# The last output product of the last token block: its K tiles in another order

## The chip, the cores and the metric

The kernel runs on one NeuronCore of one Trainium2 chip. The metric is the device time of one execution in microseconds (us), lower is better. TensorE (PE in the profile) does the matrix products into PSUM, which has eight banks of 128 x 512 float32; VectorE (DVE) and ScalarE (ACT) work on the results; GpSimd (POOL) and SyncE (SP) mostly issue transfers (DMAs) here.

## The reference

A decoder trunk of two layers on 2048 tokens of 1024 channels: an mLSTM layer, then an RG-LRU layer, each added to its input, and a last RMSNorm. The change lies in the end of the second layer. Cut to that:

```python
def rglru_mixer(u, w_in, conv_w, conv_b, w_a, b_a, w_x, b_x, lam, w_out):
    ...
    r = sigmoid(xb @ w_a + b_a)            # gates: blocks of 192 channels
    ig = sigmoid(xb @ w_x + b_x)
    log_a = -LRU_C * r * softplus(-lam)
    a = exp(log_a)
    bt = sqrt(-expm1(2.0 * log_a)) * (ig * xc)
    hs = linear_scan(a, bt)                # along the tokens
    y = hs * silu(g)                       # 1536 channels
    return y @ w_out                       # the output product: 1536 -> 1024
...
x = x + y                                  # residual
return rmsnorm(x, final_g)                 # over the 1024 channels of a token
```

## The kernel before

Phases `phase_a1`, `phase_a2` and `phase_b1` compute the mLSTM layer and the input product of the RG-LRU layer, and leave in HBM: the convolved input `xr`, the gate `g`, the residual `x1`, and the weights, already split in two. The change lies in `phase_b2`, which does the rest.

**Data.** Channels lie on the 128 partitions and tokens along the free dimension. A block is 512 tokens (`TB`), there are four (`NTB`). A float32 product is made of three matmuls in a faster format: `mm3` (L357) multiplies the high part of the weights by the high part of the data (L359), by the low part (L360), and the low part of the weights by the high part of the data (L361). High and low parts come from `split_into` (L756): a cast on ACT (L759) and a subtraction on DVE (L762).

**The two jobs.** For each block, `gates` works on four groups of 384 channels, `p` = 0 to 3. A group has six gate sums on PE (tile `gate`), tanh, exp and square root on ACT, the scan and some products on DVE, and ends with three K tiles of the data `y`, as a pair of tiles `yh` and `yl` (L1480 to L1483). So group 3 gives K tiles 9 to 11 of the output product. `x2_out` is the output product of a block, 12 K tiles (`NT`) to 1024 channels, in two halves of 512 channels. A half has four accumulators `acc` of one PSUM bank each (`m` = 0 to 3). One K tile of one half takes 12 matmuls (four `m` by the three of `mm3`) and one weight tile `wr` of 512 KB, fetched from HBM (`d_ow`). After the twelfth K tile of a half, for each `m`: the residual is loaded into `x2` on the SP queue (L1520) and the sum is added to it (L1521, DVE), it is squared (L1525 or L1528, ACT), and the squares are added up in `sacc` (L1532, DVE). After both halves, `stats_sum` (L1096) sums the squares over the channels (L1101, PE; L1104, DVE; L355, POOL), `stats_rows` (L1106) spreads the result (L1111, PE), eight products (L1547, DVE) scale the block, and it is written out (L1548).

**In the last half of the last block** K tiles 9 to 11 are held until all three are there, and are then done accumulator by accumulator, nine matmuls each, so that the accumulators end one after the other. Its last square isn't added to `sacc` but goes to `stats_sum` by itself.

**The order.** The list `steps` is written out by code: per time step one half of a group's gates, then three K tiles of the output product, five time steps (`lag`) behind. Each job is a generator, and the loop at the end of `phase_b2` resumes them in this order. In the last block's product, call the K tile steps by their place in this row, 0 to 23: places 0 to 2 stand behind the second half of the gates of group 2, places 3 to 5 and 6 to 8 behind the two halves of those of group 3, and from place 9 on there are no gates left. Before the change places 0 to 11 are K tiles 0 to 11 of half 0, and places 12 to 23 those of half 1. `weights` (L1387) hands out the weight tiles in the order of the same list, copied as `order`, and fetches up to three ahead; `wr` has four buffers, so the tile of place j goes where that of place j - 4 was. The SP queue issues in order: a transfer that has to wait holds up all behind it. `x2` has eight buffers, so a block's residual can be loaded only when the outputs of the block before it have left them.

This is the order that the code asks for. The framework's scheduler lists each engine's instructions from it, by priorities and its own idea of when things are ready, and can move an instruction ahead of its neighbours. What it made of it stands in the section on the change.

Of the kernel before, what the change touches and what calls it, by code (L numbers as in the profile page):

```python
# [14 lines left out]
P = 128  # L15
# [4 lines left out]
NTB = T // TB  # L20
# [286 lines left out]
class Trunk:  # L307
# [1052 lines left out]
    def phase_b2(self, D, outT):  # L1360
# [3 lines left out]
        NT = 12  # L1364
        with ExitStack() as ctx:
# [3 lines left out]
            pm = ctx.enter_context(tc.tile_pool(name="psB", bufs=8, space=PSUM, reuse_waits="tile"))  # L1369
            steps = []  # L1370
            lag = 5
            for t in range(8 * NTB + lag):
                if t < 8 * NTB:
                    steps.append(("g", t // 8, t % 8))
                if t >= lag:
                    steps += [("r", (t - lag) // 8, (t - lag) % 8 * 3 + i) for i in range(3)]
            order = list(steps)
            ready = []

            def fetch(kind, b, i):  # L1380

                m = 768 if kind == "g" else 512
                both = (gp if kind == "g" else wp).tile([P, 2 * m], F32R, tag="w" + kind, name="w" + kind)
                nc.sync.dma_start(both.bitcast(F32), D["gw" if kind == "g" else "ow"][i])
                return both[:, 0:m], both[:, m:2 * m]

            def weights():  # L1387

                while order and len(ready) < 3:
                    if order[0][0:2] == ("g", 0) and len(ready) == 2:  # L1390
                        break
                    with tc.high_priority(offset=80 if order[0][0:2] == ("r", 0) else None):
                        ready.append(fetch(*order.pop(0)))
                return ready.pop(0)

            def psum(name):
                return pm.tile([P, TB], F32, tag="mm", name=name)
# [101 lines left out]
            def x2_out(b):  # L1499

                bs = slice(b * TB, (b + 1) * TB)
                ys = blocks[b]
                x2, sacc = [], None
                for half in range(2):
                    acc = [psum("acc") for _ in range(4)]
                    last = b == NTB - 1 and half == 1
                    held = []
                    for k in range(NT):
                        held.append((k, weights()))
                        if not last or k < NT - 3 or k == NT - 1:  # L1510
                            for m in range(4):
                                ms = slice(m * P, (m + 1) * P)
                                for i, (wh, wl) in held:
                                    self.mm3(acc[m], wh[:, ms], wl[:, ms], ys[i][0], ys[i][1], i == 0, i == NT - 1)
                            held = []
                        if k < NT - 1:
                            yield
                    for m in range(4):
                        x = tp.tile([P, TB], F32, tag="x2", name="x2", bufs=8)
                        nc.sync.dma_start(x, D["x1"][half * 4 + m, :, bs])  # L1520
                        nc.vector.tensor_tensor(x, x, acc[m], op=ALU.add)  # L1521
                        x2.append(x)
                        if sacc is None:
                            sacc = tp.tile([P, TB], F32, tag="sacc", name="sacc", bufs=1)
                            nc.scalar.activation(sacc, x, AF.Square)  # L1525
                        else:
                            sq = tp.tile([P, TB], F32, tag="sq", name="sq")
                            nc.scalar.activation(sq, x, AF.Square)  # L1528
                            if last and m == 3:
                                sums = [sacc, sq]  # L1530
                            else:
                                nc.vector.tensor_tensor(sacc, sacc, sq, op=ALU.add)  # L1532
                                sums = [sacc]
                    yield
                rc = tp.tile([P, 4], F32, tag="rc", name="rc")
                yield
                yield
                self.stats_sum(tp, pm, sums, rc, "mm")
                yield
                yield  # L1540
                yield
                rb = self.stats_rows(pm, rc, "mm")
                if not last:
                    pb, rb = rb, tp.tile([P, TB], F32, tag="rb", name="rb", bufs=1)
                    nc.scalar.copy(rb, pb)
                for m in range(KD):
                    nc.vector.scalar_tensor_tensor(x2[m], x2[m], self.v("gf", m), rb, op0=ALU.mult, op1=ALU.mult)  # L1547
                    (nc.gpsimd if not last else nc.scalar if m % 2 else nc.sync).dma_start(outT[m, :, bs], x2[m])  # L1548
                    if m % 2:
                        yield  # L1550

            run = {}
            for kind, b, i in steps:
                if kind == "g":
                    if i == 0:
                        run["g", b] = block(b)
                    next(run["g", b])
                else:
                    if i == 0:
                        run["r", b] = x2_out(b)  # L1560
                    next(run["r", b])
                    if b > 0:
                        next(run["r", b - 1], None)
# [99 lines left out]
```

## Time and profile before

| | |
|---|---|
| time, median of 3 runs | 2966.92 us (2966.56 to 2970.99) |
| the profiled execution's own time | 2962.73 us |
| its span in the trace | 2960.7 us |
| mean granted TensorE clock in it | 0.987 of full speed |
| PE busy | 2850.7 us, 96% |
| DVE busy | 2124.2 us, 72% |
| ACT busy | 1516.8 us, 51% |

The profile is one execution, so a sum made from it is a sum against 2962.73 us, of which the trace's span covers all but 2.03 us. Times in its rows are us from the span's start, and buffer numbers are left out of names. A row of the timeline reads: start, duration, engine, line, operation, output<-inputs, count, and in brackets the engine's idle time ahead of it and what ended it. Matmuls overlap: each is shown with some 0.39 us, while the next starts 0.23 us after it. A row of the waits reads: engine, tile and line, what released it, us in total, times, the longest. In a row of the windows stand the stretch, its length, each engine's busy time with the count of its instructions, the granted clock of PE (PEclk, 1.00 is full speed), the busy share of the DMA engines and GB/s. SPq rows are transfers at the moment when SP issues them; the listing of transfers gives for each kind the count, the size and the median us from issue to landing.

### The profile page before, as it was taken

Reading aid. Unit: us, or ns where it says so; the run is one execution under the profiler, and the core shown is the slowest. Engines: PE = TensorE matmul, PEld = TensorE weight load, DVE = VectorE, ACT = ScalarE, POOL = GpSimd, SP = SyncE. Lnnn points to the kernel's source line nnn. Section 1 sums busy time; section 2 is a strip of 40 time slices with the busy share of each in tenths; the row PEclk is TensorE's granted clock in tenths of the full one; section 3 lists DMA queues with packets and bytes.
Section 4 is the critical chain, followed back from the end, with each engine's and each line's share of the span. In section 5 each row is a group of like instructions: output and inputs, shape, how many; then the busy total and the mean of one; then the engine's idle time right before and its main releaser. Section 6 shows DMA issues by size and latency. Waiting matters only on the chain.

```text
span 2960.7 us, 43267 instructions
## 1 busy us (share of the span) xinstructions
PE 2850.7 (96%) x15442; PEld 2440.3 (82%) x15442; DVE 2124.2 (72%) x3584; ACT 1516.8 (51%) x2545; POOL 445.8 (15%) x846
## 2 busy tenths in 40 slices
PE   7999999999999899999999799999999999999997
PEld 5799987889987798999999777887788887777885
DVE  7766789535668588888888755778889466766763
ACT  6354556324445466666666533435345233967761
POOL 1211122101123111111111201101221111000000
PEclk9999999999999999999999899999999999999998
DMA  6766677668889656465656568685776666878855
GB/s 228 262 227 231 239 255 269 193 200 305 267 315 314 220 166 211 142 205 171 205 185 215 213 234 285 219 264 186 257 254 210 218 199 202 293 248 306 300 193 171
DMA packets 294839, 686.58 MB, mean 232 GB/s; under 512 B 29024, under 2 KB 107616, under 8 KB 294624
## 3 DMA queue, kind: packets, MB, share of 16 engines
q1 hardware_dynamic: 227440, 450.34, 47.5%
q0 software_dynamic: 66608, 232.43, 20.9%
q8 instruction: 121, 1.98, 0.3%
q10 hardware_dynamic: 576, 1.05, 0.1%
q14 instruction: 94, 0.77, 0.1%
HBM read 446.53 MB, written 237.17 MB: 231 GB/s over the span
## 4 chain that ended last, share of the span: by engine, by line
PE 35%; DVE 12%; issue 6%; ACT 4%; DMA 1%; POOL 1%; SPq 0%; DVEq 0%; POOLq 0%; ACTq 0%
PE pa L361 2%; PE pa L359 2%; PE pa L360 2%; PE pd L360 2%; PE pd L359 2%; PE pd L361 2%; PE pc L359 2%; PE pc L360 2%; PE pc L361 2%; PE acc L360 2%; PE acc L361 2%; PE acc L359 2%; DVE Cl L762 2%; PE pb L360 1%; PE pb L361 1%
## 5 line engine op out<-in xcount | busy, mean ns | idle before, releaser
L759 ACT CAST s<-raw 128x512 fp32r<-128x512 f32 (+1 forms) x280 | 172.5, 620 | 260.6 <-PE pd L361 70.6
L762 DVE TENSOR_TENSOR s<-raw,s 128x512 fp32r<-128x512 f32 (+1 forms) x280 | 191.4, 688 | 63.9 <-ACT s L759 62.8
L359 PE MATMUL acc<-yh,wr 128*128 128x512 f32 x384 | 151.2, 402 | 15.6 <-DMA wr<-d_ow 8.3
L360 PE MATMUL acc<-yl,wr 128*128 128x512 f32 x384 | 152.8, 398 | 0.6 <-DVE yl L762 0.6
L361 PE MATMUL acc<-yh,wr 128*128 128x512 f32 x384 | 152.1, 396 | 0.0
L759 ACT CAST u<-t 128x512 fp32r<-128x512 f32 x112 | 68.8, 619 | 159.1 <-PE pc L361 49.8
L686 DVE SCALAR_TENSOR_TENSOR xc<-xm,vec,xc 128x512 f32<-128x512 f32 x192 | 139.1, 746 | 6.9 <-ACT xc L684 6.1
L762 DVE TENSOR_TENSOR u<-t,u 128x512 fp32r<-128x512 f32 x112 | 76.7, 689 | 88.4 <-ACT u L759 87.9
L759 ACT CAST s<-sum 128x512 fp32r<-128x512 f32 (+1 forms) x120 | 74.0, 618 | 117.5 <-PE pc L361 46.4
L359 PE MATMUL pa<-u,s 128*128 128x512 f32 x304 | 122.7, 403 | 4.6 <-ACT p L258 3.1
L361 PE MATMUL pa<-u,s 128*128 128x512 f32 x304 | 121.8, 401 | 0.5 <-DVE s L762 0.5
L360 PE MATMUL pa<-u,s 128*128 128x512 f32 x304 | 122.0, 401 | 0.0
L759 ACT CAST Ch<-C 128x516 fp32r<-128x516 f32 x120 | 74.8, 623 | 86.7 <-DVE da L1010 59.6
L992 DVE SCALAR_TENSOR_TENSOR C<-C,dl,kv 128x516 f32<-128x516 f32 x112 | 83.3, 744 | 47.6 <-PE kv L361 47.6
L686 DVE SCALAR_TENSOR_TENSOR xc<-xr,vec,xc 128x512 f32<-128x512 f32 x144 | 105.8, 747 | 9.2 <-ACT xc L684 8.1
L359 PE MATMUL pj<-vwh,xmh 128*128 128x512 f32 x256 | 102.6, 401 | 1.9 <-ACT vwh L759 1.8
L359 PEld LDWEIGHTS acc<-yh,wr 128*128 128x128 f32 x384 | 72.6, 190 | 36.5 <-issue 8.7
L360 PE MATMUL pj<-vwl,xmh 128*128 128x512 f32 x256 | 99.9, 390 | 1.3 <-DVE vwl L762 1.3
L762 DVE TENSOR_TENSOR s<-sum,s 128x512 fp32r<-128x512 f32 (+1 forms) x120 | 82.5, 688 | 25.6 <-ACT s L759 24.8
L361 PE MATMUL pj<-vwh,xml 128*128 128x512 f32 x256 | 100.1, 391 | 0.0
L360 PE MATMUL pd<-u,s 128*128 128x512 f32 x224 | 88.6, 395 | 1.3 <-DVE u L762 1.3
L359 PE MATMUL pd<-u,s 128*128 128x512 f32 x224 | 88.3, 394 | 0.0
(479 smaller groups left out, 10012.5 us busy)
## 6 DMA issues: line engine op xcount, KB each, us to landing
wr<-d_ow SPq DMA_DIRECT2D x96, 512.0 KB, 4.4
d_wx<-s POOLq DMA_DIRECT2D x64, 512.0 KB, 4.4
s<-d_wx SPq DMA_DIRECT2D x64, 512.0 KB, 4.4
s<-d_ws SPq DMA_DIRECT2D x64, 512.0 KB, 6.3
raw<-in_wxz_dram SPq DMA_DIRECT2D x124, 256.0 KB, 5.0
d_wr<-s POOLq DMA_DIRECT2D x48, 512.0 KB, 3.7
s<-d_wr SPq DMA_DIRECT2D x48, 512.0 KB, 4.3
wg<-d_gw SPq DMA_DIRECT2D x32, 768.0 KB, 4.9
```

Of the source, the lines that this page charges most:

```text
L359: mm(out, sh, mh, start=first, stop=False, skip_group_check=resumed)
L360: mm(out, sh, ml, start=False, stop=False, skip_group_check=resumed)
L361: mm(out, sl, mh, start=False, stop=last, skip_group_check=resumed)
L686: nc.vector.scalar_tensor_tensor(out, x[:, j:j + TB], self.v(wn, m * 4 + j), out, op0=ALU.mult, op1=ALU.add)
L759: a = nc.scalar.copy(hi, src)
L762: b = (nc.gpsimd if lo_eng == "p" else nc.vector).tensor_tensor(lo, src, hi.bitcast(F32), op=ALU.subtract)
L992: nc.vector.scalar_tensor_tensor(C2, C2, self.dl[:, r:r + 1], p2, op0=ALU.mult, op1=ALU.add)
```

## The change

In the last block the output product takes its K tiles in the order: tiles 0 to 8 of half 0 (places 0 to 8, as before), tiles 0 to 8 of half 1 (places 9 to 17), tiles 9 to 11 of half 0 (18 to 20), tiles 9 to 11 of half 1 (21 to 23, held as before). `turn` maps the place to half and K tile. Both halves' accumulators are then open at once, eight banks, and the end of half 0 (residual, squares, sums) comes right ahead of half 1's held tiles. The other blocks keep their order. No instruction is added or left out.

```diff
+            def turn(b, i):
+
+                if b < NTB - 1 or i < NT - 3:
+                    return i
+                return i + 3 if i < 2 * NT - 6 else i - (NT - 3) if i < 2 * NT - 3 else i
...
-                    steps += [("r", (t - lag) // 8, (t - lag) % 8 * 3 + i) for i in range(3)]
+                    steps += [("r", (t - lag) // 8, turn((t - lag) // 8, (t - lag) % 8 * 3 + i)) for i in range(3)]
...
-                for half in range(2):
-                    acc = [psum("acc") for _ in range(4)]
-                    last = b == NTB - 1 and half == 1
-                    held = []
-                    for k in range(NT):
-                        held.append((k, weights()))
-                        if not last or k < NT - 3 or k == NT - 1:
-                            for m in range(4):
-                                ms = slice(m * P, (m + 1) * P)
-                                for i, (wh, wl) in held:
-                                    self.mm3(acc[m], wh[:, ms], wl[:, ms], ys[i][0], ys[i][1], i == 0, i == NT - 1)
-                            held = []
-                        if k < NT - 1:
-                            yield
+                last = b == NTB - 1
+                accs = {}
+                held = []
+                for j in range(2 * NT):
+                    half, k = divmod(turn(b, j), NT)
+                    if k == 0:
+                        accs[half] = [psum("acc") for _ in range(4)]
+                    acc = accs[half]
+                    held.append((k, weights()))
+                    if not last or half == 0 or k < NT - 3 or k == NT - 1:
+                        for m in range(4):
+                            ms = slice(m * P, (m + 1) * P)
+                            for i, (wh, wl) in held:
+                                self.mm3(acc[m], wh[:, ms], wl[:, ms], ys[i][0], ys[i][1], i == 0, i == NT - 1)
+                        held = []
+                    if k < NT - 1:
+                        yield
+                        continue
...
-                            if last and m == 3:
+                            if last and half == 1 and m == 3:
```

What the scheduler made of it, first on PE at place 9 (the numbers tell buffers apart: `wr_28106` is the weight tile of place 9 in both kernels, `wr_28156` before that of place 12; `acc_27902` to `acc_27905` are half 0, `acc_28207` to `acc_28210` half 1 before, `acc_28142` to `acc_28145` half 1 after; `yh_28084` and `yl_28085` are the data of group 3, `yh_27534` and `yl_27535` of group 0). Before:

```order
L361 MATMUL acc_27905<-yh_27898,wr_28088 128x512
L359 MATMUL acc_28207<-yh_27534,wr_28156 128x512
L359 MATMUL acc_27902<-yh_28084,wr_28106 128x512
L359 MATMUL acc_27903<-yh_28084,wr_28106 128x512
L359 MATMUL acc_27904<-yh_28084,wr_28106 128x512
L360 MATMUL acc_27902<-yl_28085,wr_28106 128x512
L361 MATMUL acc_27902<-yh_28084,wr_28106 128x512
```

After:

```order
L361 MATMUL acc_27905<-yh_27898,wr_28088 128x512
L359 MATMUL acc_28142<-yh_27534,wr_28106 128x512
L360 MATMUL acc_28142<-yl_27535,wr_28106 128x512
L361 MATMUL acc_28142<-yh_27534,wr_28106 128x512
L359 MATMUL acc_28143<-yh_27534,wr_28106 128x512
L360 MATMUL acc_28143<-yl_27535,wr_28106 128x512
```

Before, one matmul of place 12 stood ahead of place 9, and behind it place 9, which reads group 3. Now place 9 is the first K tile of half 1, which reads group 0, and the places follow each other in their own order up to the last.

On SP the places of the transfers stay the same, and only what is fetched changes. From the weight tile of place 9 to that of place 13, before (`x2` is the residual, half 0's from `x2_28184`, half 1's from `x2_28375`):

```order
L1384 DMA wr_28106<-d_ow_95 128x1024
L1520 DMA x2_28184<-d_x1_85 128x512
L1520 DMA x2_28189<-d_x1_85 128x512
L1520 DMA x2_28195<-d_x1_85 128x512
L1520 DMA x2_28201<-d_x1_85 128x512
L1384 DMA wr_28124<-d_ow_95 128x1024
L1520 DMA x2_28375<-d_x1_85 128x512
L1384 DMA wr_28142<-d_ow_95 128x1024
L1520 DMA x2_28381<-d_x1_85 128x512
L1520 DMA x2_28387<-d_x1_85 128x512
L1384 DMA wr_28156<-d_ow_95 128x1024
L1520 DMA x2_28393<-d_x1_85 128x512
```

After:

```order
L1390 DMA wr_28106<-d_ow_95 128x1024
L1530 DMA x2_28314<-d_x1_85 128x512
L1530 DMA x2_28319<-d_x1_85 128x512
L1530 DMA x2_28325<-d_x1_85 128x512
L1530 DMA x2_28331<-d_x1_85 128x512
L1390 DMA wr_28124<-d_ow_95 128x1024
L1530 DMA x2_28375<-d_x1_85 128x512
L1390 DMA wr_28146<-d_ow_95 128x1024
L1530 DMA x2_28381<-d_x1_85 128x512
L1530 DMA x2_28387<-d_x1_85 128x512
L1390 DMA wr_28160<-d_ow_95 128x1024
L1530 DMA x2_28393<-d_x1_85 128x512
```

The tiles of places 9 to 12 are `wr_28106`, `wr_28124`, `wr_28142` (after: `wr_28146`) and `wr_28156` (after: `wr_28160`), in this order in both. The residual loads stand between them as before.

On DVE, the end of half 0 and the first accumulator of half 1 (`x2_28375`). Before:

```order
L1521 TENSOR_TENSOR x2_28201<-x2_28201,acc_27905 128x512
L1532 TENSOR_TENSOR sacc_28187<-sacc_28187,sq_28192 128x512
L1532 TENSOR_TENSOR sacc_28187<-sacc_28187,sq_28198 128x512
L1532 TENSOR_TENSOR sacc_28187<-sacc_28187,sq_28204 128x512
L1521 TENSOR_TENSOR x2_28375<-x2_28375,acc_28207 128x512
L1532 TENSOR_TENSOR sacc_28187<-sacc_28187,sq_28378 128x512
```

After:

```order
L1531 TENSOR_TENSOR x2_28331<-x2_28331,acc_27905 128x512
L1542 TENSOR_TENSOR sacc_28317<-sacc_28317,sq_28322 128x512
L1542 TENSOR_TENSOR sacc_28317<-sacc_28317,sq_28328 128x512
L1531 TENSOR_TENSOR x2_28375<-x2_28375,acc_28142 128x512
L1542 TENSOR_TENSOR sacc_28317<-sacc_28317,sq_28334 128x512
L1542 TENSOR_TENSOR sacc_28317<-sacc_28317,sq_28378 128x512
```

One addition to `sacc` has gone behind the first addition of half 1; the rest stands as before. ACT and POOL keep their order.

## The prediction

> **What bounds the kernel now.** I read the page first, then PE's waits over the whole span, then the timeline and the windows around the one wait that lies in the changed product.
>
> ```profile
> span 2960.7 us, 43267 instructions
> PE 2850.7 (96%) x15442; PEld 2440.3 (82%) x15442; DVE 2124.2 (72%) x3584; ACT 1516.8 (51%) x2545; POOL 445.8 (15%) x846
> ...
> PE pt L1045 <- ACT hh L1035: 13.9, 3, 11.7
> PE ssum L1101 <- DVE acc L498: 13.6, 1, 13.6
> PE acc L359 <- DMA wr<-d_ow: 8.3, 1, 8.3
> ```
>
> PE is busy for 96% of the span, so time comes from what PE waits for and from nothing else, unless the end is touched. The third wait is the output product's, and it happened once. The two above it lie in other phases. In PE's timeline the wait is this:
>
> ```profile
> 2892.72 0.40 PE L361 MATMUL acc<-yh,wr 128*128 128x512 f32 x1
> 2901.41 2.04 PE L359 MATMUL acc<-yh,wr 128*128 128x512 f32 x4 [8.29 <-DMA wr<-d_ow]
> ...
> 2904.41 0.39 PE L361 MATMUL acc<-yh,wr 128*128 128x512 f32 x1
> ...
> 2944.38 0.40 PE L361 MATMUL acc<-yh,wr 128*128 128x512 f32 x1
> ```
>
> The row at 2892.72 is the last matmul of place 8. The order of before has behind it one matmul of place 12 and then place 9, so PE stood for two things at once: the weights of place 12 and the data of group 3. The two engines that make that data, and the SP queue with the weights:
>
> ```profile
> 2897.36 1.47 ACT L759 CAST yh<-g 128x1536 fp32r<-128x1536 f32 x1 [1.60 <-DVE g L1479]
> ...
> 2898.87 1.76 DVE L762 TENSOR_TENSOR yl<-g,yh 128x1536 fp32r<-128x1536 f32 x1 [1.54 <-ACT yh L759]
> ...
> 2860.76 19.31 SPq L1384 DMA_DIRECT2D wr<-d_ow  x6
> 2885.18 3.79 SPq L1520 DMA_DIRECT2D x<-d_x  x4
> 2889.07 0.40 SPq L1384 DMA_DIRECT2D wr<-d_ow  x1
> 2890.36 0.32 SPq L1520 DMA_DIRECT2D x<-d_x  x1
> 2890.78 0.45 SPq L1384 DMA_DIRECT2D wr<-d_ow  x1
> 2891.57 2.55 SPq L1520 DMA_DIRECT2D x<-d_x  x2
> 2894.21 0.38 SPq L1384 DMA_DIRECT2D wr<-d_ow  x1
> 2895.66 0.32 SPq L1520 DMA_DIRECT2D x<-d_x  x1
> 2906.00 27.97 SPq L1384 DMA_DIRECT2D wr<-d_ow  x11
> ```
>
> The group of six ends with the tile of place 9, issued at about 2879.7; the three single ones are places 10, 11 and 12; the eleven are places 13 to 23. The listing of transfers gives their times to landing, for places 9, 10, 11 and 12 in this order, and the last row is that of all issued from 2895 on:
>
> ```profile
> wr<-d_ow SPq DMA_DIRECT2D x1, 512.0 KB, 3.4
> ...
> wr<-d_ow SPq DMA_DIRECT2D x1, 512.0 KB, 7.7
> ...
> wr<-d_ow SPq DMA_DIRECT2D x1, 512.0 KB, 7.9
> ...
> wr<-d_ow SPq DMA_DIRECT2D x1, 512.0 KB, 7.1
> ...
> DMA to landing us min/median/max: 3.4/3.6/5.1
> ```
>
> So place 9 landed at 2883.1, place 10 at 2896.8, place 11 at 2898.7 and place 12 at 2894.21 + 7.1 = 2901.3. PE went on at 2901.41, 0.1 us behind that last one: the weights of place 12 ended the wait. But the data was hardly earlier: `yh` was there at 2898.83, `yl` at 2900.63.
>
> **What goes.** The stretches of that product by windows, of the instructions on `acc` alone:
>
> ```profile
> 2884.60:2893.00 8.40, 8.40 (x36) 6.59 (x35) 0.00 (x0) 0.00 (x0) 1.00 0.91 288
> 2893.00:2901.40 8.40, 0.12 (x1) 0.02 (x1) 0.00 (x0) 0.00 (x0) 0.76 0.93 354
> 2901.40:2904.40 3.00, 2.99 (x7) 2.40 (x8) 0.00 (x0) 0.00 (x0) 0.52 0.00 0
> 2904.40:2944.80 40.40, 40.38 (x174) 32.40 (x172) 4.81 (x7) 0.00 (x0) 1.00 0.46 143
> ```
>
> First the pause. In the first window 36 matmuls take 8.40 us, 0.233 each, so place 9 could have begun at 2892.72 + 0.23 = 2892.95. It began at 2901.41: 8.46 us. Second, the clock behind the pause: for 3.00 us PE was granted 0.52 of full speed, which costs 3.00 x 0.48 = 1.44 us. A second way to the same number: places 9 to 23 are 180 matmuls, 41.9 us at 0.233 each, and took from 2901.41 to 2944.61, 43.2 us. Together 9.9 us hang on this wait.
>
> **What comes.** After the change place 9 needs only the weights that landed at 2883.1 and data of group 0, which is long there; its four banks were last read by the gates on ACT, the last of them here:
>
> ```profile
> 2884.79 0.69 ACT L1441 ACTIVATE ig<-gate,lc 128x512 f32<-128x512 f32 x1
> ```
>
> That ends at 2885.5, 7 us before. So place 9 runs from 2892.95 to 2895.74 (12 x 0.233). Place 10 needs weights that were issued behind four residual loads and landed at 2896.8; PE went on 0.1 us behind a landing above, so it starts at 2896.87: a new wait of 1.13 us. Nothing about that transfer changes, since SP's places are the same and up to 2892.95 all engines do what they did. I take 1.13 us. Behind it on PE stand only the places that follow, and DVE and ACT have nothing of this product to do until half 0 ends, so the wait moves the end by its own length. Its bounds: nothing, if the load takes the 3.4 us of place 9's (landing at 2892.5), and 1.3 us if it takes place 11's 7.9.
>
> [...]
>
> Places 11 and 12 come at 2896.87 + 2.79 = 2899.66 and 2902.45, and their weights are there at 2898.7 and 2901.3. The loads of places 13 and 14 move forward: SP waited with them for a free buffer, and places 9 and 10 now free theirs at some 2896 and 2899.8. Landing after 3.6 to 7.9 us, they are there from 2899.6 to 2903.9 and from 2903.4 to 2907.7; PE wants them at 2905.24 and 2908.03. That holds, but at the long end by 1.3 and 0.3 us only, which is where I look for trouble. From place 15 on the stretch is quiet again (median 3.6) and a tile has three K tiles of time, 8.4 us. The last tile is issued at 2906.00 + 27.97 - 0.32 = 2933.65 before and lands at 2937.25, and the held matmuls want it at 2944.61 - 30 x 0.233 = 2937.6; its distance to the tiles ahead of it doesn't change, so neither does that. Half 0's residuals are loaded as early as before and only wait longer in their buffers, which nobody wants any more.
>
> What a short wait does to the clock shows in an earlier place, where the data of the group before came late:
>
> ```profile
> 2797.37 1.20 PE L359 MATMUL acc<-yh,wr 128*128 128x512 f32 x4 [0.90 <-ACT yh L759]
> 2798.41 0.39 PE L360 MATMUL gate<-xcl,wg 128*128 128x512 f32 x1
> ```
>
> Four matmuls take 1.04 us instead of 0.93: 0.1 us behind a pause of 0.90. I take 0.1 here too.
>
> Group 3's data is wanted at place 18, at 2892.95 + 1.13 + 0.1 + 9 x 2.79 = 2919.3, 18.7 us behind `yl`. Even if the gates' chain got slower by that much, it would cost nothing.
>
> **The end.** Half 0's end now lies right ahead of half 1's. What DVE does in both, before:
>
> ```profile
> 2909.49 2.77 DVE L1521 TENSOR_TENSOR x<-x,acc 128x512 f32<-128x512 f32 x4 [8.87 <-PE acc L361]
> 2912.19 2.28 DVE L1532 TENSOR_TENSOR sacc<-sacc,sq 128x512 f32<-128x512 f32 x3
> 2938.55 0.69 DVE L1521 TENSOR_TENSOR x<-x,acc 128x512 f32<-128x512 f32 x1 [24.08 <-PE acc L361]
> 2939.99 0.69 DVE L1532 TENSOR_TENSOR sacc<-sacc,sq 128x512 f32<-128x512 f32 x1 [0.76 <-ACT sq L1528]
> 2940.63 0.69 DVE L1521 TENSOR_TENSOR x<-x,acc 128x512 f32<-128x512 f32 x1
> ...
> 2944.82 0.69 DVE L1521 TENSOR_TENSOR x<-x,acc 128x512 f32<-128x512 f32 x1
> ```
>
> Half 0's last accumulator was done at about 2911.5; DVE had its four additions behind it 0.7 us later and the first two of `sacc` 2.0 us later. Half 1's first accumulator is done 9 x 0.233 = 2.1 us later, when DVE is just free for it. From there on a round of DVE is 2940.63 - 2938.55 = 2.08 us, and PE's nine matmuls are 2.1 us, so the two keep step as before; the addition to `sacc` that was put behind the first addition of half 1 fills the 0.76 us in which DVE waited for ACT. So the end costs 0 to 0.1 us. Its other bound is a slip by one addition and its wait, 0.69 + 0.76 = 1.45 us, since a chain without slack never makes good a delay. Everything behind 2944.82 is as before.
>
> **Sum.** -8.46 - 1.44 + 1.13 + 0.1 + 0.1 = -8.6 us. Against the profiled execution's own 2962.73 us (span 2960.7) that is 2954.1. The median of the three runs is 4.2 us above the profiled one, by something that the profile doesn't show; applied to the median the forecast is 2966.92 - 8.6 = 2958.3 us, -0.29%. About 0.2%, 5.9 us, is what a measurement of this kernel can tell from no change.
>
> **Rivals.**
>
> A second wait behind the first. If the forward moved loads of places 13 and 14 land later than any seen here, because they join the crowded stretch earlier, PE waits again. With 7.9 + 3.6 = 11.5 us for place 13, issued at 2896, it lands at 2907.5 and costs 2.3 us: -6.3 us. If that pause also brings the slow clock, 1.44 us more: -4.9 us, 2962.0, no difference that can be told. For it speaks the margin of 0.3 us; against it that the traffic that made 7.9 us ends by itself (the window from 2901.40 on has no transfer at all). Chance 0.14.
>
> A shorter pause in ordinary runs. The profiled execution may have had place 12's weights late. But without that, place 9 of before still had to wait for `yh` at 2898.83: a pause of 5.9 us at least. Then -5.9 - 1.44 + 1.13 = -6.2 us or a little more, 2960.7. It also covers that the wait was put down to the wrong thing: whichever of weights or data it was, it goes. Chance 0.12.
>
> The end slips by one step: -8.6 + 1.4 = -7.2 us, 2959.7. Chance 0.06.
>
> Slower: the clock. If several short waits in a row (places 10, 13, 14) brought PE to the 0.52 seen behind the long pause, again and again, half of the 168 matmuls from place 10 on would take 1.92 times as long: 84 x 0.233 x 0.92 = 18 us more, and -8.6 becomes +9.4, 2976.3. All of them would be 36 us; slower by over 0.2% begins at 8.6 + 5.9 = 14.5 us of loss, with 40% of them slow. Against it: behind the 0.90 us pause the rows show 0.1 us of loss, and the windows 1.00 with PE busy throughout. [...] Chance 0.03.
>
> **How the numbers follow.** The forecast as worked out has what is left, 0.65. Faster by over 0.2%: nearly all of that (0.62), most of the slipping end (0.05), and about half of the shorter pause and a third of the second wait (0.11): 0.78. Slower by over 0.2%: the clock and a little that I don't see, 0.04. The rest, 0.18, is no difference. The range: at the low end 9.8 us, all that goes and no new wait, against the profiled execution's own time, 2952.9; at the high end the second wait with the slow clock, 2962.0, and 1 us of the runs' scatter: 2953 to 2963.
>
> **What would show it.** Right: in PE's waits the 8.3 us for `wr` is gone, and one of some 1.1 us stands near 2895.8; PEclk is 1.00 from 2893 on; PE's last matmul on `acc` starts near 2935.8 instead of 2944.38; DVE's last addition follows it within 0.1 us. Wrong: a wait of over 2 us on `wr` at places 13 or 14, a clock below 0.9 between 2893 and 2935, a gap between PE's last matmul and DVE's last addition, or a span that shrinks by less than 6 us.

## The result, and the profile after

Over five runs each, the changed kernel took 2956.82 us in the median (2954.88 to 2958.55) against 2966.92 us (2965.79 to 2972.34) for the one before: a ratio of 0.9965, with an interval of 0.9954 to 0.9975. It is faster by 0.35%. Run again later beside other kernels, it came to 2954.07 us and a ratio of 0.9961 (0.9949 to 0.9974). The forecast was 2958.3 us, faster.

The page of the kernel after: span, engines and the clock granted to TensorE.

```profile
span 2955.1 us, 43268 instructions
...
PE 2851.6 (96%) x15442; PEld 2440.9 (83%) x15442; DVE 2124.6 (72%) x3584; ACT 1517.0 (51%) x2545; POOL 445.5 (15%) x846
...
PEclk9999999999999999999999999999999999999999
```

PE's busy time is what it was (2850.7 before). The span is 5.6 us shorter, so waiting went away and not work. PE's waits in the last 255 us (columns: who waited for what, sum, times, longest):

```profile
PE acc L359 <- ACT yh L759: 0.9, 1, 0.9
PE acc L359 <- DMA wr<-d_ow: 0.9, 2, 0.6
```

The one wait of 8.3 us for weights has become two that make 0.9 us together; the wait for `yh` lies in an earlier block and stands in both kernels. PE's timeline has the two new ones, and the first and last row of the stretch that the change reaches:

```profile
2895.40 0.39 PE L361 MATMUL acc<-yh,wr 128*128 128x512 f32 x1
...
2898.19 0.39 PE L361 MATMUL acc<-yh,wr 128*128 128x512 f32 x1
...
2899.19 0.50 PE L359 MATMUL acc<-yh,wr 128*128 128x512 f32 x1 [0.61 <-DMA wr<-d_ow]
2899.53 0.39 PE L360 MATMUL acc<-yl,wr 128*128 128x512 f32 x1
...
2931.94 0.50 PE L359 MATMUL acc<-yh,wr 128*128 128x512 f32 x1 [0.29 <-DMA wr<-d_ow]
...
2938.78 0.40 PE L361 MATMUL acc<-yh,wr 128*128 128x512 f32 x1
```

2895.40 is the last matmul of place 8. Place 9 follows it without a gap and ends with the matmul at 2898.19; place 10 begins at 2899.19, behind its weights. The row at 2931.94 is where the held tiles begin (places 21 to 23). From here on I measure the changed product by one number, **the stretch**: from the start of place 8's last matmul to the start of the last matmul on the accumulators. 180 matmuls lie in it, 41.8 us at their usual distance of 0.232. Before, it was 2944.38 - 2892.72 = 51.66 us; after, 2938.78 - 2895.40 = 43.38 us. That is 8.28 us gained.

The window over the stretch (us, then busy time of PE, PEld, DVE and ACT, the clock, the DMA engines' share, GB/s) shows what became of the stage at 0.52:

```profile
2895.60:2939.10 43.50, 42.60 (x181) 33.47 (x179) 4.82 (x7) 0.00 (x0) 1.00 0.59 201
```

Full clock throughout. The tile of place 10 in SP's queue, its landing, and the transfers issued from 2898 on (min, median, max):

```profile
2887.86 4.04 SPq L1530 DMA_DIRECT2D x<-d_x  x4
2892.00 0.60 SPq L1390 DMA_DIRECT2D wr<-d_ow  x1
...
2898.61 29.18 SPq L1390 DMA_DIRECT2D wr<-d_ow  x11
```

```profile
wr<-d_ow SPq DMA_DIRECT2D x1, 512.0 KB, 7.1
...
DMA to landing us min/median/max: 4.1/4.3/7.2
```

2892.00 + 7.1 = 2899.1, and PE went on at 2899.19. The tile of place 23 is the last of the eleven: issued at 2898.61 + 29.18 - 0.32 = 2927.47 (its issue took 0.32), wanted by the held tiles, which went on at 2931.94, 4.5 us behind the issue. The end, on DVE:

```profile
2934.39 0.69 DVE L1542 TENSOR_TENSOR sacc<-sacc,sq 128x512 f32<-128x512 f32 x1 [0.16 <-ACT sq L1538]
2935.04 0.69 DVE L1531 TENSOR_TENSOR x<-x,acc 128x512 f32<-128x512 f32 x1
2936.49 0.69 DVE L1542 TENSOR_TENSOR sacc<-sacc,sq 128x512 f32<-128x512 f32 x1 [0.76 <-ACT sq L1538]
...
2939.22 0.69 DVE L1531 TENSOR_TENSOR x<-x,acc 128x512 f32<-128x512 f32 x1
```

DVE's last addition starts 0.04 us behind PE's last matmul (2938.78 + 0.40). From PE's last matmul on `acc` to the end of the span there are 16.3 us before and after (16.6 when the changed kernel was run again).

One thing doesn't fit at first sight: the stretch lost 8.28 us, the span 5.6. The rest lies ahead of the stretch, in instructions that the change leaves in place: place 8 ended 2.68 us later than in the execution before. One of the waits that differ there, in the time up to 2885 us, of before and of after:

```profile
PE acc L359 <- ACT ig L1441: 0.7, 2, 0.4
```

```profile
PE acc L359 <- ACT ig L1447: 2.3, 2, 1.9
```

In all eleven experiments, some built from the kernel before and some from the one after, this wait is 2.1 to 2.3 us. So the 0.7 of before was luck in the one execution that was profiled. Over the thirteen profiles place 8's last matmul starts anywhere from 2891.1 to 2896.9 us. That scatter of 5.8 us, not the change, makes spans of single executions differ, and it is why the experiments are read by the stretch first.

### The profile page after: what moved, and what is told of

Its sections match the earlier page's. It is cut to its first block, busy times and chain, and to the rows that moved or that the text cites. A ratio compares the mean times of both kernels' runs of the same rounds, so it can differ in the third digit from the quotient of the medians.

```text
span 2955.1 us, 43268 instructions
## 1 busy us (share of the span) xinstructions
PE 2851.6 (96%) x15442; PEld 2440.9 (83%) x15442; DVE 2124.6 (72%) x3584; ACT 1517.0 (51%) x2545; POOL 445.5 (15%) x846
## 4 chain that ended last, share of the span: by engine, by line
PE 35%; DVE 12%; issue 6%; ACT 4%; DMA 1%; POOL 1%; DVEq 0%; POOLq 0%; SPq 0%; ACTq 0%
PE pa L361 2%; PE pa L359 2%; PE pa L360 2%; PE pd L360 2%; PE pd L359 2%; PE pd L361 2%; PE pc L359 2%; PE pc L360 2%; PE pc L361 2%; PE acc L360 2%; PE acc L361 2%; PE acc L359 2%; DVE Cl L762 2%; PE pb L360 1%; PE pb L361 1%
```

## The experiments

**The theory.** In the kernel before, PE stood behind place 8 for two things on top of each other: the data of group 3, and, through one matmul of place 12 that the scheduler had put ahead of place 9, the weights of place 12. The data is the cause, and the change works because nine tiles lie between. The first rival is that the weights are the cause, late because SP put residual loads ahead of them. The second is that the slow clock behind the pause comes from something other than the idle time, so that it would be there without it. All ratios are to runs of the kernel before on the same chip.

| kernel | stretch, us | ratio (interval) |
|---|---|---|
| before (its profile) | 51.66 | 1 |
| before, place 12's matmul in its place | 50.87 | 0.9997 (0.9988 to 1.0007) |
| before, 36 more matmuls in the pause | 50.25 | 0.9997 (0.9987 to 1.0006) |
| before, residual loads late | 48.13 | 0.9990 (0.9981 to 1.0000) |
| before, data of group 3 not needed | 42.98 | 0.9971 (0.9961 to 0.9980) |
| after, one tile of half 1 first | 46.76 | 0.9987 (0.9978 to 0.9996) |
| after, three tiles of half 1 first | 42.62 | 0.9968 (0.9956 to 0.9980) |
| after | 43.38 | 0.9965 (0.9954 to 0.9975) |
| after, run again | 43.14 | 0.9961 (0.9949 to 0.9974) |
| after, residual loads late | 41.83 | 0.9968 (0.9957 to 0.9979) |
| the same, run again | 41.83 | 0.9971 (0.9960 to 0.9981) |
| after, five weight buffers | 41.83 | 0.9954 (0.9940 to 0.9968) |
| after, residual loads late, five buffers | 41.83 | 0.9959 (0.9946 to 0.9971) |

**1. Before, without the early matmul of place 12.** It is tied behind the last matmul of place 11 (`mm3` here returns its first and its last matmul, and `order` puts the second argument behind the first).

```diff
+ a = self.mm3(acc[m], wh[:, ms], wl[:, ms], ys[i][0], ys[i][1], i == 0, i == NT - 1)
+ if b == NTB - 1 and (half, i) == (1, 0):
+     self.order((ended,), a[0:1])
+ if half == 0:
+     ended = a[1]
```

> The kernel before, with an order set between two matmuls: the first of place 12 may not stand ahead of place 11's last. Nothing else moves. I read the stretch S from the start of place 8's last matmul to the start of the product's last one: 51.66 us before, 43.38 after the change, 41.8 (180 x 0.232) without any wait. My theory is that place 9 stood for two things at nearly the same time, the weights of place 12 (8.7 us behind place 8) and the data of group 3 (6.2 us behind it). Then taking the early matmul away wins the difference only: a pause of some 6.0 us for the ACT cast and the slow clock behind it, S = 41.8 + 6.0 + 1.4 = 49.2, 2.5 us less than before. Rival, the weights alone: places 9 to 11 have theirs in time but for some 1 us, S = 42 to 44. Rival, the data alone: no change, 51.7.

PE's timeline where the pause ends, and the windows behind it:

```profile
2902.46 2.07 PE L359 MATMUL acc<-yh,wr 128*128 128x512 f32 x4 [5.77 <-ACT yh L760]
```

```profile
2902.40:2904.50 2.10, 2.04 (x5) 1.41 (x6) 0.00 (x0) 0.00 (x0) 0.50 0.81 322
2904.50:2906.00 1.50, 1.50 (x5) 1.21 (x5) 0.00 (x0) 0.00 (x0) 0.50 0.05 18
2906.00:2910.00 4.00, 4.00 (x13) 3.11 (x13) 0.00 (x0) 0.00 (x0) 0.67 0.19 47
2910.00:2947.50 37.50, 37.50 (x162) 29.88 (x160) 4.81 (x7) 0.00 (x0) 1.00 0.48 149
```

Without the weights the wait stays, now for `yh`, and is 2.5 us shorter, as expected. But the stretch gained only 0.8 us, since the slow clock lasted until some point between 2906 and 2910, where it had lasted 3.0 us. From 2902.46 on the 179 distances took 44.71 us instead of 41.56: 3.15 us lost to the clock, against 1.41 before by the same working. The rival by which the weights alone hold PE is out.

**2. Before, with data that is there.** In half 0 of the last block, K tiles 9 to 11 read the data of K tiles 0 to 2. Thus 512 channels of 512 tokens aren't the reference's.

```diff
- self.mm3(acc[m], wh[:, ms], wl[:, ms], ys[i][0], ys[i][1], i == 0, i == NT - 1)
+ y = ys[i - 9 if b == NTB - 1 and half == 0 and i > 8 else i]
+ self.mm3(acc[m], wh[:, ms], wl[:, ms], y[0], y[1], i == 0, i == NT - 1)
```

> The kernel before, in the old order, but in the last block K tiles 9 to 11 of half 0 multiply the data of K tiles 0 to 2 in place of their own, so 512 output channels of 512 tokens aren't the reference's; the work and the transfers are the same. PE then never has to wait for group 3 at place 9. Theory: this alone gives what the change gave, S (from place 8's last matmul to the product's last) = 43.4, with one short wait of 0.6 to 1.1 us for the weights of place 10, some 10 us less than before in the runs. Rival, that it was the new place of half 0's end or the order of the weights that gave the gain: S stays near 51.

The only wait that PE has in the stretch:

```profile
2897.46 0.50 PE L359 MATMUL acc<-yh,wr 128*128 128x512 f32 x1 [0.73 <-DMA wr<-d_ow]
```

42.98 us, without any change of the order. The scheduler no longer put a matmul of place 12 ahead either. That fits its having stood there only because the scheduler saw nothing else ready for PE; no run shows its reasons. So the data is the cause of both waits, and the 0.73 us at place 10 are the wait that the change meets with 0.61.

**3. Before, with the residual loads late**, behind the weight load of place 13 (`wloads` collects the weight loads in their order).

```diff
+ if kind == "r":
+     wloads.append(d)
...
- nc.sync.dma_start(x, D["x1"][half * 4 + m, :, bs])
+ d = nc.sync.dma_start(x, D["x1"][half * 4 + m, :, bs])
+ if b == NTB - 1:
+     self.order((wloads[b * 2 * NT + 13],), (d,))
```

> The kernel before, with the eight residual loads of the last block put behind the weight load of place 13 on the SP queue, so that the weights of places 10 to 12 aren't queued behind them. The early matmuls of place 12 stay ahead of place 9 (four of them now). Theory: the weights of place 12 then come before the data of group 3, and PE waits for the cast at 6.2 us behind place 8; the four early matmuls take 0.9 us of the pause; the slow clock still comes: S = 41.8 + 5.1 + 1.4 = 48.3, 3.4 us less than before. Rival, the weights alone: S = 42 to 43. Rival, the data alone: 51.7 less at most 0.9.

```profile
2895.97 0.47 PE L359 MATMUL acc<-yh,wr 128*128 128x512 f32 x1 [4.35 <-DMA wr<-d_ow]
...
2896.85 2.61 PE L359 MATMUL acc<-yh,wr 128*128 128x512 f32 x5
```

The size came out as expected (48.13), the wait not quite: with no residual load ahead of it, place 12's tile still held PE for 4.35 us. With four buffers it takes the one of place 8, so it can't be issued before place 8 is done: it was issued at 2891.65, 0.4 us behind the start of place 8's last matmul, and landed 4.2 us later. With these buffers the early matmul couldn't have been free by any order of the loads. The size came out because the data still came last: `yh` was there at 2897.33, behind the weights. The rest of the stretch above 41.8 us is again the slow clock (0.66 from 2896 to 2901 in its window).

**4. Before, with the pause filled.** Behind place 8 of half 0 come 36 matmuls into a spare bank, on weights and data of the last gates; nothing reads their result.

```diff
+ if b == NTB - 1 and half == 0 and k == 8:
+     fh, fl, dh, dl = self.fill
+     ps = psum("fill")
+     for i in range(12):
+         ws = slice(i % 6 * P, (i % 6 + 1) * P)
+         self.mm3(ps, fh[:, ws], fl[:, ws], dh[:, i % 3], dl[:, i % 3], i == 0, i == 11)
```

> The kernel before with 36 added matmuls behind place 8, on weights and data of the last gates that lie in SBUF, into a spare bank that nobody reads. They take 8.4 us, about the pause, so places 9 to 23 start when they did, but PE has not stood still. Theory: the granted clock stays at 1.00 and the 1.44 us that the slow start cost are gone: S = 41.8 + 8.4 = 50.2 with the filler in it, 1.4 us less than before in spite of 36 matmuls more. Rival, that the slow matmuls behind the pause were slow for another reason (their operands, the banks): S = 51.6.

Two windows on all instructions (POOL's busy time stands behind ACT's): 8.4 us of filling, then the first 3 us of place 9 on.

```profile
2894.80:2903.20 8.40, 8.40 (x38) 6.91 (x37) 6.09 (x5) 1.68 (x2) 0.00 (x0) 1.00 0.94 347
2903.20:2906.20 3.00, 3.00 (x15) 2.41 (x14) 0.00 (x0) 0.00 (x0) 0.00 (x0) 1.00 0.03 5
```

Where PE had been granted 0.52 behind the pause, it has 1.00 behind filled time, and the stretch is 1.4 us shorter though PE does nothing for it in those 8.4 us. So the slow clock hung on the idle time, and the forecast's -1.44 is a term of its own. As a remedy it can't be told from no change by the runs: ratio 0.9997.

**5 and 6. The change with one tile of half 1 ahead, and with three**, instead of nine.

```diff
- return i + 3 if i < 2 * NT - 6 else i - (NT - 3) if i < 2 * NT - 3 else i
+ return i + 3 if i < NT - 3 + 1 else i - 1 if i < NT + 1 else i
```

For three, 3 stands for 1 in each of the three places.

> The change with less cover: only one K tile of half 1 goes ahead of half 0's K tiles 9 to 11 in place of nine. Theory: cover counts by its time against the data's lateness. Place 9 takes 2.8 us, then PE stands for the cast until 6.2 us behind place 8 (3.2 us), does four matmuls and stands for the subtraction until 8.0 (0.9 us): S (from place 8's last matmul to the product's last; 51.66 before, 43.38 after) = 41.8 + 4.1 = 45.9, and 47.3 if so short a pause already brings the slow clock. Rival, that the gain comes only from the scheduler no longer taking a matmul of place 12 first: 43 to 44.

> The change with three K tiles of half 1 ahead of half 0's last three. Theory: three tiles are 8.4 us, more than the 8.0 us that the data is late, so S is that of the change, 43.4, and half 0 ends where it ended before, far ahead of half 1's end; the time from the product's last matmul to the end of the span is 16.3 us as in both. So three tiles do what nine do, within 0.3 us. Rival, that half 0's end so close to half 1's costs something in the change: c3 is up to 1.4 us faster behind the last matmul.

One tile, PE's timeline and windows:

```profile
2902.70 1.92 PE L359 MATMUL acc<-yh,wr 128*128 128x512 f32 x4 [2.98 <-ACT yh L759]
```

```profile
2899.60:2902.70 3.10, 0.12 (x1) 0.00 (x0) 0.00 (x0) 0.00 (x0) 1.00 1.03 404
2902.70:2907.00 4.30, 4.29 (x11) 3.06 (x12) 0.00 (x0) 0.00 (x0) 0.60 0.64 255
```

Three tiles, PE's one wait, and DVE where half 0 ends and half 1 begins to:

```profile
2896.37 0.51 PE L359 MATMUL acc<-yh,wr 128*128 128x512 f32 x1 [0.51 <-DMA wr<-d_ow]
```

```profile
2908.53 2.77 DVE L1531 TENSOR_TENSOR x<-x,acc 128x512 f32<-128x512 f32 x4 [7.95 <-PE acc L361]
...
2929.45 0.69 DVE L1531 TENSOR_TENSOR x<-x,acc 128x512 f32<-128x512 f32 x1 [15.95 <-PE acc L361]
```

One tile covers 2.8 us, and PE stands 2.98 us for `yh`, with the slow clock behind it: 46.76, between the two values expected (45.9 without the slow clock, 47.3 with it). Three tiles cover 8.4 us, more than the 7.9 that the data takes, and the wait is gone: 42.62, 0.8 us below what I expected, mostly because the short wait at the held tiles isn't there. Six more tiles bring nothing. With three, half 0 ends 20.9 us ahead of half 1, where the change puts the two ends side by side; both profiled executions have 16.3 us behind PE's last matmul, so the place of half 0's end costs nothing there.

**7. After, with the residual loads late**, behind the weight load of place 14; the edit is that of experiment 3 with 14 for 13.

> The changed kernel, with the last block's residual loads behind the weight load of place 14 on the SP queue. Theory: the wait of 0.61 us at place 10 came from weights behind the residual loads in a crowded stretch; without them it goes, S = 43.38 - 0.8 = 42.6, and the runs are 0 to 1 us below the changed kernel's. Rival, that the outputs of the block before make the transfers slow: the wait stays or shrinks little. Risk: residuals between the later weights make PE wait there, S above 43.4.

SP's queue: thirteen weight tiles in a row, up to place 14, then the residuals begin. Below it PE's window.

```profile
2849.44 48.00 SPq L1390 DMA_DIRECT2D wr<-d_ow  x13
2897.53 0.86 SPq L1532 DMA_DIRECT2D x<-d_x  x2
```

```profile
2891.00:2933.30 42.30, 42.30 (x183) 33.99 (x181) 4.81 (x7) 0.00 (x0) 1.00 0.64 209
```

PE is busy for all of the window, and the stretch is at its floor, 0.8 us below what I expected: the short wait at the held tiles went too. So both waits that the change leaves go once the weight tiles up to place 14 stand ahead of the residuals on SP. By the runs it is no faster than the change (0.9968).

**8. The same with five weight buffers** instead of four.

```diff
- wp = ctx.enter_context(tc.tile_pool(name="w4", bufs=4, reuse_waits="tile"))
+ wp = ctx.enter_context(tc.tile_pool(name="w4", bufs=5, reuse_waits="tile"))
```

> As the changed kernel with late residual loads, and with five weight buffers in place of four. The change's second wait, 0.29 us, stood at the held tiles, for the weights of place 23, whose buffer came free only with place 19. Theory: with five that load can start 2.8 us earlier and the wait is gone: S = 42.0 to 42.3, without any wait on weights. Rival: no difference from four buffers.

The stretch is 41.83 us, as in 7: nothing was left for a buffer to gain.

**9 to 11, on one chip: the change again, with five buffers alone, and with the residual loads late again.**

> The change as it is, again, on the same chip as the next two. Expected by all theories: 0.996 to 0.997 of before, and 43.4 us (43.0 to 43.8) from the last matmul of place 8 to the last one on the accumulators, with waits of 0.5 to 1.1 us at place 10.

> The change with five weight buffers, the residual loads left where they stand on SP. Theory (the wait at place 10 comes from SP's order: the tile is issued behind four residual loads, which had a pause of 5 us ahead of them): the wait at place 10 stays, 42.8 to 43.6 us in the stretch; the short one at the held tiles goes, since those tiles are issued a place earlier. Rival (the load waits for a weight buffer): no wait at all, 41.8 us. By the runs' medians neither can be told from the change.

> The change with the residual loads behind the weight load of place 14, beside the change on the same chip. Theory: no wait, 41.8 us in the stretch, 1.5 us less than the change; a median 1 to 2 us lower, 0.9995 of it, with intervals that overlap. Rival (the 1.5 us are given back behind the stretch): the same median as the change, and more than 16.3 us from the last matmul on the accumulators to the end of the span.

Five buffers alone, SP's queue around the residual loads:

```profile
2851.51 29.03 SPq L1390 DMA_DIRECT2D wr<-d_ow  x8
2885.65 4.06 SPq L1530 DMA_DIRECT2D x<-d_x  x4
...
2896.40 25.41 SPq L1390 DMA_DIRECT2D wr<-d_ow  x10
```

I had expected place 10's tile to stay behind the four residual loads. It didn't: ten tiles stand in the last row where the change has eleven, since with a fifth buffer each tile is issued one place earlier, and place 10's now goes ahead of the residuals. The stretch is 41.83 us without a wait, so the rival of that run was right and the buffer alone does it.

By the runs, the three can't be told apart: 2954.07, 2953.04 and 2957.05 us, with overlapping intervals. The third has 1.3 us less in its stretch than the first and 3 us more in its median, where I had expected 1 to 2 us less. Behind its last matmul it has the same 16.3 us (2955.0 - 2938.75), so the gain isn't given back there. But place 8's last matmul started at 2896.92 in its profiled execution, and at 2891.75 in the change's. That scatter lies ahead of the stretch and is larger than the gain. The version with five buffers has the lowest ratio of all (0.9954); better than the change it is in its trace only.

## Why the prediction was right, and where not

**The pause (-8.46).** Right. Place 9 follows place 8 without a gap. Experiment 2 shows the data as the cause, experiment 1 that the weights were only the later of two waits, as the prediction said.

**The clock (-1.44).** Right as a term (experiment 4), and right in this execution. As a size it is not firm: 1.4 us behind the pause of 8.3, 3.15 behind one of 5.8, and 1.8 behind one of 3.0 (from 2902.70 to the last matmul at 2943.30, 40.60 us for 167 distances that take 38.78; a short wait for `yl` is in it). That it was as little as 1.4 in the execution before looks like chance: more than half of the slow time (4.0 of 6.8 us) fell into the pause, and the slow time began at no fixed distance behind PE's last matmul (3.6 to 5.5 us, see the last section). The rival "a shorter pause" counted 1.44 behind a pause of 5.9; in the one execution with such a pause (5.77) it was 3.15.

**The new wait at place 10 (+1.13, and +0.1 for the restart).** Right in mechanism, too big. From 2898.19 to 2899.19 there is 1.00 us instead of 0.23, and the next distance is 0.34: 0.88 us in all. SP issued the tile 3.4 us ahead of place 8's last matmul (2895.40 - 2892.00), where before it was 3.65 (2892.72 - 2889.07), and it took 7.1 us instead of 7.7. So it landed 3.7 us behind that matmul and not 4.05.

**Places 13 and 14.** No wait. Place 13's tile was issued at 2898.61 and took 7.2 us, so it was there at 2905.8, 1.9 us before PE wanted it (2899.19 + 3 x 2.79 + 0.11 = 2907.7). Place 14's took 4.8 us from 2902.28 and was 3.4 us early. The margins feared at the long end were 1.3 and 0.3 us.

**The held tiles (0).** This is the step that failed: "its distance to the tiles ahead of it doesn't change, so neither does that". The distance held, but the loads of that stretch took 4.3 us in the middle where they had taken 3.6, and the margin of 0.35 us was gone: from the matmul ahead of it to 2931.94 there are 0.69 us, then 0.34, 0.57 us lost. Run again, it lost 0.40, and the loads took 4.2 us again. With three tiles ahead, with late residuals and with five buffers they took 3.5 us in the middle there, and PE didn't wait. So the longer loads go with this kernel and not with one execution; why it has them stays open.

**The end (+0.1).** It cost nothing: 16.3 us in both kernels, and as much with three tiles ahead. The 16.6 us of the second run and the 17.2 of experiment 1, a kernel with the old order, have another source: the small matmuls that sum the squares (`ssum`) took longer. In experiment 1 the last of them follow each other at 0.43 us, from 2949.92 on, where it is 0.22 before; in the second run DVE waited 2.96 us for `ssum`, where it waited 2.61 before.

**The sum.** -8.46 - 1.44 + 0.88 + 0.57 is -8.45 us for the stretch, where 8.28 were measured and 8.5 the second time; forecast were -8.67, and -8.6 with the end. Most of the 0.17 us between lies in the undisturbed distances, 0.2331 us each after and 0.2323 before. That the forecast's new waits were 0.35 us too large in one place and 0.57 too small in the other, and nearly cancel, is luck. The rivals "a second wait", "the end slips" and "slower: the clock" didn't happen; PE had 1.00 throughout the stretch.

**The median.** The prediction set a span that shrinks by less than 6 us as a sign that it is wrong, and the span shrank by 5.6. That sign was badly chosen: the scatter ahead of the stretch is as large as the gain. For the same reason the 4.2 us between the profiled execution and the median of before were no fixed offset but the scatter of executions; the profile of before shows one of the shorter ones. The runs' own difference, 10.1 us by the medians with an interval of 7 to 14 (0.0025 to 0.0046 of 2967), holds the 8.3 us.

## What to carry to other kernels

When an in-order engine waits, look at what else would be waiting there once the named wait is gone; here the second was 2.6 us earlier than the first (2898.83 and 2901.41), and edits that took away or shortened the first one alone gained 0.8 and 3.5 us of nearly 10. Work that covers a wait has to be as long as the latest data is late, and no longer: here the data was 7.9 us late, three tiles (8.4 us) did what nine did, and one (2.8 us) did about half. Where the gain is smaller than the scatter of the executions, measure the stretch that the change reaches, from one fixed instruction to another, and let the runs only confirm it.

## What the runs showed of the hardware

What a pause cost through the clock wasn't set by its length: 1.4 us behind 8.3 us before, 3.15 behind 5.8 in experiment 1, 1.8 behind 3.0 in experiment 5. The granted clock in windows laid close around its steps, before:

```profile
2892.72:2897.40 4.68, 0.40 (x2) 0.00 (x0) 0.00 (x0) 0.00 (x0) 1.00 1.02 380
2897.50:2904.20 6.70, 2.79 (x7) 2.24 (x8) 0.00 (x0) 0.00 (x0) 0.50 0.49 190
2904.30:2907.00 2.70, 2.70 (x14) 2.18 (x13) 0.00 (x0) 0.00 (x0) 1.00 0.08 6
```

In experiment 1:

```profile
2896.30:2901.70 5.40, 0.40 (x2) 0.00 (x0) 0.00 (x0) 0.00 (x0) 1.00 1.02 375
2901.90:2908.60 6.70, 6.14 (x14) 4.63 (x15) 0.00 (x0) 0.00 (x0) 0.50 0.35 137
2908.70:2911.00 2.30, 2.30 (x11) 1.85 (x10) 0.00 (x0) 0.00 (x0) 1.00 0.69 224
```

Half speed was granted for some 6.8 us in both. Before, it began at 2897.45 and PE went on at 2901.41, so 4.0 us of it passed in the pause and 2.8 us fell on work, which at half speed lose 1.4. In experiment 1 it began at 2901.8 and PE went on at 2902.46, so 6.2 us fell on work and lose 3.1. In experiments 3 and 5 half speed lasted 3.4 us (2896.6 to 2900.0, and 2902.9 to 2906.3; the windows have 0.66 over 5.0 us and 0.60 over 4.3) and began only after PE had gone on, at 2895.97 and 2902.70. It came 4.7, 5.5, 5.4 and 3.6 us behind the start of PE's last matmul ahead of the pause (before, experiments 1, 3 and 5), so at no fixed time. Behind waits of 0.3 to 0.9 us it didn't come: the windows have 1.00 behind the 0.29 and 0.61 us of after, the 0.73 of experiment 2 and the 0.90 before (at 2797.37). Half speed lasted some 6.8 us in two of these executions and half as long, 3.4 us, in two; what decides between them isn't shown.

The loads of 512 KB that were issued from 2860 us on, before and after, took 3.4 to 4.4 us where 0.4 to 0.7 of the DMA engines' time was taken between issue and landing, and 6.9 to 8.0 us where it was 0.92 to 1.03. Two don't fit this: 5.1 us at 0.71 (before, issued at 2911.6) and 4.8 us at 0.95 (after, place 14). PE went on about 0.1 us behind the landing that it waited for (2901.3 and 2901.41 before, 2899.1 and 2899.19 after).
